# Fourier front of a two-layer encoder: where the even halves of the mixer's output are added, and when the third even weight is split

## The chip, the cores and the metric

The kernel runs on one core of a Trainium2 chip. The time is the device time of the whole program in microseconds (us), as a median of several runs. The profile is of one execution. Its engines are PE (TensorE matmuls), PEld (TensorE weight loads), DVE (VectorE), ACT (ScalarE), POOL (GpSimd) and SP (SyncE, which here only issues transfers). L12 is line 12 of the kernel that the profile shows.

## The reference

Two sequences of 512 tokens with 1024 features go through two layers. Layer 0 mixes tokens by a 2-D Fourier transform, layer 1 by grouped attention; each is followed by a squared-ReLU MLP. The change lies in layer 0's mixer.

```python
def fourier_mix(h, w_out):
    B, S, _ = h.shape
    hg = h.astype(jnp.float32).reshape(B, S, N_FGROUPS, F_GROUP)
    f = jnp.fft.fft2(hg, axes=(1, 3), norm="ortho").real
    f = f.reshape(B, S, D_MODEL).astype(h.dtype)
    return f @ w_out

def trunk(x, ...):
    for i in range(DEPTH):
        if i % N_MIXERS == 0:
            x = x + fourier_mix(rms_norm(x, fourier_norm[j]), fourier_w_out[j])
        else:
            x = x + gqa_attention(rms_norm(x, attn_norm[j]), ...)
        x = x + sq_relu_mlp(rms_norm(x, mlp_norm[i]), mlp_w_up[i], mlp_w_down[i])
    return rms_norm(x, final_norm)
```

All of it is float32. Most products split each operand into a rounded high part and the rest, the low part, and take three matmuls (high x high, high x low, low x high).

## The kernel before

The front (layer 0's mixer) is written out by hand: inside `tc.manual_schedule` each engine runs its instructions in the order of the code, and waits only for data, buffers and transfers. PE first transforms sequence 0, then takes its products with the output weight, transforms sequence 1 (`transform`) and takes its products, and then starts layer 0's MLP, whose first products are at L1039. After that nothing is part of the change.

The transform's result is symmetric in the tokens up to a sign, so the product with the weight falls into an even half (257 token columns, from the sums of weight rows, `we`) and an odd half (255 columns, from the differences, `wo`). Output column n gets even + odd, its mirror column, n + 256 in the kernel's token order, even - odd. A `Fold` j = 0 to 3 makes a quarter of these weights: `minus` forms the difference on DVE and adds the other rows into the raw weight by an accumulating transfer (POOL L694), `even_hi` casts the sum to its high part (ACT L711), and `even_lo` subtracts for the low part (DVE L714).

The residual `xs[q, i]` holds feature tiles 2i and 2i+1 of sequence q, one pair, [128, 2, 512]. For sequence 0 it is put together in steps:

- `odd_put` copies an odd product from PSUM into the pair, plain (ACT L777) and negated into the mirrored columns (L778).
- `add_input` adds the layer's input to the pair by an accumulating transfer on POOL's queue (L801), pairs in the order 2, 0, 3, 1.
- `even_put` copies the even product from PSUM to `even_part[i]` (ACT L786); for pairs 0 and 1 it copies a second time into the mirrored columns (L788).
- `add_even` adds `even_part[i]` to the pair: pairs 0 and 1 by an accumulating transfer from SBUF to SBUF (POOL L793), pairs 2 and 3 on DVE (L796, which reads the even half twice through a broadcast, and L798 for the two edge columns).

Accumulating transfers into one pair have to wait for each other. Between the folds and the input adds stand POOL's L440 transfers, which fold sequence 1's own input (after DVE's L431 and L444). When a pair is complete, `square` squares its tiles on ACT (L180) and POOL adds them up (L184). PE reduces the sum over the partitions (`root`, L193), DVE and ACT make the inverse root (L141 to L146), and PE spreads it over the partitions (`spread`, L201, copied by ACT L202) for the MLP's norm.

Sequence 1's transform calls `hook1` after each sequence part ("seq", 0 to 3) and feature stage ("feat", 0 to 3); its order is seq 0, 1, 2, feat 0, seq 3, feat 1, 2, 3. After each part its result is split by ACT and DVE at L86 and L87, the high part by ACT and the low part by DVE, which also sets PSUM banks free. The last split of the transform is `nyq_out` (ACT L596, DVE L597), which the last matmul (L754) of each even product reads. `hook1` places the squares, the later pair adds, sequence 1's loads (`load_xs`, SP L168, held until the square given as `made` is done) and the first put-aways (L214) and MLP weight loads (L101) among these steps. Sequence 1's even products then go to `xs[1, i]` by DVE (L765, L766), after which the odd ones follow (L770, L771).

Of the kernel before, what the change touches and what calls it, by code (L numbers as in the profile page):

```python
# [16 lines left out]
ALU = mybir.AluOpType  # L17
# [27 lines left out]
def trunk_kernel(ctx, tc, x_in, xt_in, y_out, tables, rope, gfour, gcol, grow, gfin,  # L45
                 w_four, w_nyq, w_qkv, w_o, w_a22, w_up, w_row2, w_row4, w_sum2, w_sum4, w_down):
    nc = tc.nc
# [17 lines left out]
    def slot(shape, dt):  # L65
        return act.tile(shape, dt, tag="u4", name=nm("u"))

    def tm(shape=(P, 512), dt=F32):
        return tmp.tile(list(shape), dt, tag="t2", name=nm("t"))
# [29 lines left out]
    def load_raw(src, shape=(P, 1024)):  # L99
        raw = rawp.tile(list(shape), F32, tag="raw", name=nm("raw"))  # L100
        nc.sync.dma_start(raw, src)  # L101
        return raw
# [62 lines left out]
    def load_xs(q, src, after=None):  # L165
        for i in range(4):
            xs[q, i] = slot([P, 2, 512], F32)
            made = nc.sync.dma_start(xs[q, i], src[i])  # L168
            if after is not None:
                behind(made, after, sync=True)  # L170

    def xt(q, fo):
        return xs[q, fo // 2][:, fo % 2]

    def square(q, fo, n=512, alone=False, first=0):

        if fo == first:
            acc[q] = tm()
        s = acc[q] if fo == first else tm()
        made = nc.scalar.activation(s[:, :n], xt(q, fo)[:, :n], AF.Square)  # L180
        if alone:
            apart[q] = s
        elif fo != first:
            nc.gpsimd.tensor_add(acc[q][:, :n], acc[q][:, :n], s[:, :n])  # L184
        return made
# [27 lines left out]
    def put_away(q, i):  # L213
        nc.sync.dma_start(park[q, i], xs[q, i])  # L214
# [542 lines left out]
    def even_outs(q, fos):  # L757
        return outs(q, fos, we, 0, 258, (wn.w, un[q]))

    def odd_outs(q, fos):  # L760
        return outs(q, fos, wo, 256, 256)
# [13 lines left out]
    def odd_put(q, fo, o):  # L775
        x = xt(q, fo)
        nc.scalar.copy(x[:, 1:256], o[:, 1:256])  # L777
        nc.scalar.activation(x[:, 257:], o[:, 1:256], AF.Copy, scale=-1.0)  # L778

    even_part = {}  # L780

    def even_put(q, fo, o):
        i, f = fo // 2, fo % 2
        if f == 0:
            even_part[i] = slot([P, 2, 512], F32)
        nc.scalar.copy(even_part[i][:, f, :257], o[:, :257])  # L786
        if i < 2:
            nc.scalar.copy(even_part[i][:, f, 257:], o[:, 1:256])  # L788

    def add_even(q, i):  # L790
        x, e = xs[q, i], even_part[i]
        if i < 2:
            nc.gpsimd.dma_start(x, e, accum_op=ALU.add)  # L793
            return
        both = x.rearrange("p f (h n) -> p f h n", h=2)[:, :, :, 1:]
        nc.vector.tensor_add(both, e[:, :, 1:256].unsqueeze(2).broadcast_to([P, 2, 2, 255]), both)  # L796
        edge = x[:, :, 0:257:256]
        nc.vector.tensor_add(edge, e[:, :, 0:257:256], edge)  # L798

    def add_input(q, i):  # L800
        nc.gpsimd.dma_start(xs[q, i], xt_in[q][i], accum_op=ALU.add)  # L801

    ET = mybir.EngineType
    with tc.manual_schedule(engines={ET.PE, ET.Activation, ET.DVE, ET.Pool, ET.SP}):
# [19 lines left out]
        fold = [Fold(0)]  # L824
# [63 lines left out]
        order = [4, 5, 6, 7, 0, 1, 2, 3]  # L888
        o = dict(zip(order, odd_outs(0, order)))
# [12 lines left out]
        fold[1].even_hi()  # L902
        fold[1].even_lo()
        g0.chain(5, 6)
        for fo in order[:2]:
            odd_put(0, fo, o[fo])
        for j in range(2, 4):
            fold[j].even_hi()
            fold[j].even_lo()
        g0.gain(1)  # L910
        g0.minus(1)
        g0.plus_there(1)
        for fo in order[2:]:
            odd_put(0, fo, o[fo])
        for i in range(2):
# [5 lines left out]
        g1.gain(1)  # L921
        g1.minus(1)
        g1.plus_there(1)
        for i in (2, 0, 3, 1):
            add_input(0, i)
        g1.squares(1)
        g1.chain(1, 2)
        e = even_outs(0, range(3))
        for fo in range(2):
            even_put(0, fo, e[fo])  # L930
        add_even(0, 0)

        def even(fo):
            even_put(0, fo, even_outs(0, [fo])[0])
# [6 lines left out]
        g0.split_odd()  # L941
        g1.chain(4, 6)
        even_put(0, 2, e[2])
        for i in range(2):
            g1.scale(slice(i, i + 1))
        even(3)
        add_even(0, 1)
        even(4)
        g1.combine()
        g1.split_hi()  # L950
        g1.split_lo()
        for fo in range(5, KC):
            even(fo)
        add_even(0, 2)

        raws = []
        blocks = Blocks(0)

        def hook1(at, j):
            if at == "seq":  # L960
                if j < 3:
                    made = square(0, order[j], first=4)
                if j == 0:
                    add_even(0, 3)
                elif j == 1:
                    load_xs(1, xt_in[1], made)
                    put_away(0, 2)
                    raws.extend(load_raw(w_up[0, 2 * p]) for p in range(4))
            else:
                square(0, order[3 + j], first=4)  # L970
                if j == 3:
                    square(0, order[7], first=4)

        transform(1, hook1)
        for fo in range(KC):
            e, = even_outs(1, [fo])
# [561 lines left out]
    def qkv(cg, q, t, ws, k0=0, k1=KC, o=None):  # L1538
        o = ps() if o is None else o
        cols = slice(t * P, (t + 1) * P)  # L1540
        for k in range(k0, k1):
            w = ws[k // 2]
            c = (k % 2) * 512
            mm3(o, hT[q][k][:, 0, cols], hT[q][k][:, 1, cols],
                w[0][:, c : c + 512], w[1][:, c : c + 512], k == 0, k == KC - 1)
        return o
# [62 lines left out]
    def transpose_q(q, h):  # L1609
        pt = ps()  # L1610
        c = (h % 2) * HD
        for t in range(NT):
            nc.tensor.transpose(pt[:, t * P : (t + 1) * P], qr[q, h // 2][:, t, c : c + HD], ident)  # L1613
        qT = slot([P, 2, 512], F32R)
        split(qT[:, 0], qT[:, 1], pt)
        return qT
# [150 lines left out]
    with tc.manual_schedule(engines={ET.Activation, ET.DVE}):  # L1767
        for cg in (2, 0, 1):
            later = next_ws({2: 0, 0: 1}[cg]) if cg != 1 else iter(())
            for q in range(NSEQ):  # L1770
# [6 lines left out]
                for t in range(NT if (cg, q) != (1, 1) else 2):  # L1777
                    if (cg, q, t) == (1, 1, 0):
                        first = transpose_q(0, 0)
# [19 lines left out]
    with tc.manual_schedule(engines={ET.Activation}):  # L1799
        o = qkv(1, 1, 2, ws[1])  # L1800
# [6 lines left out]
        o = qkv(1, 1, 3, ws[1])  # L1807
# [34 lines left out]
    todo, e, rows = heads_out.plain_sums(), [tm() for _ in range(4)], []  # L1842
# [13 lines left out]
    with tc.manual_schedule(engines={ET.PE}):  # L1856
        o = {}
# [12 lines left out]
        o = {}  # L1870
# [24 lines left out]
        o, lows = {}, []  # L1895
# [89 lines left out]
    with tc.manual_schedule(engines={ET.PE, ET.Activation, ET.DVE, ET.Pool, ET.SP}):  # L1985
# [17 lines left out]
        x, z = xtok  # L2003
# [3 lines left out]
        def tile(t, c0, c1, at=0, mid=lambda: None):  # L2007
            o = ps()[:, : c1 - c0]
            for k in range(len(ats)):
                ak, wk = ats[k][1], ws[k]  # L2010
                cols = slice(t * P, (t + 1) * P)
                mm3(o, ak[0][:, cols], ak[1][:, cols], wk[0][:, c0:c1], wk[1][:, c0:c1], k == 0, k == len(ats) - 1)
                if k == at:
                    mid()
            return o
# [11 lines left out]
        o = [tile(2, 0, 512, 2, ob.root)]  # L2027
# [8 lines left out]
        o = [tile(3, 0, 512)]  # L2036
# [183 lines left out]
```

## Time and profile before

| | |
|---|---|
| runs | 1683.16, 1678.90, 1682.27 us; median 1682.27 us |
| profiled execution | 1682.66 us, span 1680.9 us, mean granted clock 0.998 |
| busy, share of the span | PE 1662.8 us (99%), PEld 83%, DVE 75%, ACT 52%, POOL 23% |
| chain that ended last | PE 93%, DMA 2%, DVE 2%, ACT 1%, issue 1% |
| input adds L801 | 4 transfers of 512 KB, issued from 48.6 to 55.7 us |
| even transfers L793 | 2 of 512 KB, issued at 59.2 and 64.7 us, landing after 8.7 and 10.3 us |
| first MLP product (L1039) | starts at 100.86 us |

A timeline row has the start, the length, the engine, the line, the operation, out<-in, shapes and a count; in brackets stands how long the engine was idle before it and what is held to have ended that. A landing is the time from a transfer's issue to its end. The releaser of a wait is inferred: where the one named had long been done, it was another, often a transfer.

### The profile page before, as it was taken

The numbers are of one execution on the slowest core, as the hardware profiler recorded it, in microseconds if no ns is written. First come the engines' busy times: TensorE is split into PE (matmuls) and PEld (weight loads), VectorE is DVE, ScalarE is ACT, GpSimd is POOL, SyncE is SP. The second block draws the span as 40 slices with busy tenths as digits, with TensorE's granted clock in tenths as the row PEclk, the third lists the DMA queues.
The fourth block names the chain that finished last, engine by engine and source line by source line (L and its number), as shares of the span: only waits on it lengthen the run. The fifth ranks groups of instructions, "written<-read, shape, count | busy, mean of one in ns | idle before, by whom it ended". The sixth has DMA issues, their size and how long they took to land.

```text
span 1680.9 us, 22279 instructions
## 1 busy us (share of the span) xinstructions
PE 1662.8 (99%) x7827; PEld 1387.0 (83%) x7827; DVE 1265.0 (75%) x1855; ACT 873.2 (52%) x1546; POOL 394.5 (23%) x370
## 2 busy tenths in 40 slices
PE   9899999999999999999999999999999999999998
PEld 8788888888888888888888888888888888888887
DVE  8579787446877869868888977777855487878875
ACT  7665445446442435437688855554544552433334
POOL 3420543231000000424544312004422220000002
PEclk9999999999999999999999999999999999999999
DMA  9942555449865757525501146334544696756632
GB/s 311 268 146 85 201 188 184 167 168 336 298 224 162 232 171 236 187 72 173 188 14 39 64 163 225 123 116 160 210 155 156 221 375 198 234 159 217 192 105 101
DMA packets 122480, 303.53 MB, mean 181 GB/s; under 512 B 12376, under 2 KB 13528, under 8 KB 122368
## 3 DMA queue, kind: packets, MB, share of 16 engines
q1 hardware_dynamic: 98720, 253.53, 43.5%
q0 software_dynamic: 9248, 22.10, 6.3%
q10 hardware_dynamic: 14400, 26.48, 4.2%
q8 instruction: 61, 1.00, 0.2%
q14 instruction: 51, 0.42, 0.1%
HBM read 217.59 MB, written 82.38 MB: 178 GB/s over the span
## 4 chain that ended last, share of the span: by engine, by line
PE 93%; DMA 2%; DVE 2%; ACT 1%; issue 1%; POOL 0%; SPq 0%; DVEq 0%; POOLq 0%; ACTq 0%
PE ps L1039 73%; PE ps L81 6%; PE ps L83 6%; PE ps L82 6%; PE ps L1634 2%; DMA u<-u 1%; DMA u<-xt 1%; DMA u<-x 0%; PE ps L1613 0%; PE ps L193 0%; DMA raw<-w_sum 0%; DMA u<-spill_t 0%; DVE u L431 0%; DVE u L87 0%; ACT u L86 0%
## 5 line engine op out<-in xcount | busy, mean ns | idle before, releaser
L1039 PE MATMUL ps<-u,w 128*128 128x512 f32 x4944 | 1131.1, 389 | 0.0
L1039 PEld LDWEIGHTS ps<-u,w 128*128 128x128 f32 x4944 | 926.5, 188 | 195.1 <-ACT u L1072 1.7
L86 ACT CAST w<-raw 128x1024 fp32r<-128x1024 f32 (+1 forms) x216 | 213.6, 994 | 310.4 <-PE ps L1039 234.9
L87 DVE TENSOR_TENSOR w<-raw,w 128x1024 fp32r<-128x1024 f32 (+1 forms) x216 | 252.1, 1171 | 75.1 <-ACT w L86 74.8
L86 ACT CAST u<-u 128x1024 fp32r<-128x1024 f32 (+1 forms) x140 | 140.7, 1046 | 84.1 <-PE ps L1039 40.2
L87 DVE TENSOR_TENSOR u<-u,u 128x1024 fp32r<-128x1024 f32 (+1 forms) x140 | 169.0, 1237 | 18.8 <-ACT u L86 18.4
L1039 PE MATMUL ps<-u,u 128*128 128x512 f32 x600 | 143.4, 390 | 0.3 <-DVE t L1249 0.3
L1276 POOL DMA_DIRECT2D raw<-w_sum x32 | 27.7, 866 | 469.0 <-DVE w L87 143.1
L1249 DVE TENSOR_TENSOR u<-ps,u 128x512 f32<-128x512 f32 x160 | 109.8, 688 | 37.0 <-PE ps L1039 34.5
L1157 POOL TENSOR_TENSOR u<-u 128x512 f32<-128x512 f32 x28 | 37.1, 1326 | 424.7 <-ACT u L1054 424.7
L1039 PEld LDWEIGHTS ps<-u,u 128*128 128x128 f32 x600 | 112.5, 188 | 24.5 <-DVE t L1249 0.7
L81 PE MATMUL ps<-u,u 128*128 128x512 f32 (+2 forms) x340 | 128.8, 381 | 2.8 <-DVE u L87 2.2
L184 POOL TENSOR_TENSOR t<-t,t 128x512 f32<-128x512 f32 (+1 forms) x54 | 79.4, 1474 | 190.0 <-ACT t L180 189.0
L83 PE MATMUL ps<-u,u 128*128 128x512 f32 (+2 forms) x340 | 123.8, 365 | 0.0
L82 PE MATMUL ps<-u,u 128*128 128x512 f32 (+2 forms) x340 | 123.7, 365 | 0.0
L1053 ACT ACTIVATE t<-t 128x512 f32<-128x512 f32 x64 | 40.5, 632 | 110.9 <-DVE t L1126 100.8
L81 PEld LDWEIGHTS ps<-u,u 128*128 128x128 f32 x340 | 64.4, 189 | 11.2 <-DVE u L87 1.8
L87 DVE TENSOR_TENSOR u<-ps,u 128x512 fp32r<-128x512 f32 (+3 forms) x112 | 68.0, 635 | 6.6 <-ACT u L86 6.0
L83 PEld LDWEIGHTS ps<-u,u 128*128 128x128 f32 x340 | 64.2, 189 | 10.5 <-DVE u L87 0.2
L82 PEld LDWEIGHTS ps<-u,u 128*128 128x128 f32 x340 | 64.4, 189 | 8.5 <-DVE u L87 0.5
L1113 DVE TENSOR_TENSOR t<-ps,u 128x512 f32<-128x512 f32 x32 | 22.1, 689 | 59.9 <-PE ps L1039 52.4
L180 ACT ACTIVATE t<-u 128x512 f32<-128x512 f32 (+1 forms) x64 | 37.9, 602 | 54.2 <-DVE u L1846 21.0
(282 smaller groups left out, 2051.7 us busy)
## 6 DMA issues: line engine op xcount, KB each, us to landing
raw<-w_up SPq DMA_DIRECT2D x80, 512.0 KB, 4.6
u<-spill_t SPq DMA_DIRECT2D x60, 512.0 KB, 6.8
raw<-w_sum SPq DMA_DIRECT2D x56, 512.0 KB, 5.4
u<-spill_b SPq DMA_DIRECT2D x45, 512.0 KB, 6.6
spill_t<-u SPq DMA_DIRECT2D x84, 256.0 KB, 2.0
spill_b<-t ACTq DMA_DIRECT2D x60, 256.0 KB, 4.4
raw<-w_row SPq DMA_DIRECT2D x28, 512.0 KB, 5.0
park<-u SPq DMA_DIRECT2D x24, 512.0 KB, 4.7
```

Source lines behind the costliest of these rows:

```text
L81: nc.tensor.matmul(out, lh, rh, start=first, stop=False)
L82: nc.tensor.matmul(out, lh, rl, start=False, stop=False)
L83: nc.tensor.matmul(out, ll, rh, start=False, stop=last)
L86: hi = nc.scalar.copy(dst_hi, src)
L87: return hi, eng.tensor_sub(dst_lo, src, f32(dst_hi))
L180: made = nc.scalar.activation(s[:, :n], xt(q, fo)[:, :n], AF.Square)
L184: nc.gpsimd.tensor_add(acc[q][:, :n], acc[q][:, :n], s[:, :n])
L1039: nc.tensor.matmul(o, w[x][:, sl], h[k][y], start=first and k + i == 0, stop=k == n - 1 and i == 2, skip_group_check=not first)
L1053: nc.scalar.activation(t, src, AF.Relu)
L1157: eng.tensor_sub(t[:, 0], b12, b11)
L1249: return nc.vector.tensor_add(x, o, x)
L1634: nc.tensor.transpose(pt[:, t * P : (t + 1) * P], probs[t][:, sc * P : (sc + 1) * P], ident)
```

## The change

`even_put` makes one copy for all pairs, and `add_even` adds all pairs on DVE; the two L793 transfers and the four L788 copies are gone. Pairs 0 and 1 are added after feat 0 and seq 3 of sequence 1's transform, among the low parts. The input adds go in the order 2, 3, 0, 1. Sequence 1's loads and what follows them on SP move from after seq 1 to after feat 0. The third even weight is split ahead of the first odd copies, the fourth behind the next gain and fold of sequence 1's input.

```diff
     def even_put(q, fo, o):
...
         nc.scalar.copy(even_part[i][:, f, :257], o[:, :257])
-        if i < 2:
-            nc.scalar.copy(even_part[i][:, f, 257:], o[:, 1:256])

     def add_even(q, i):
         x, e = xs[q, i], even_part[i]
-        if i < 2:
-            nc.gpsimd.dma_start(x, e, accum_op=ALU.add)
-            return
         both = x.rearrange("p f (h n) -> p f h n", h=2)[:, :, :, 1:]
...
         g0.chain(5, 6)
+        fold[2].even_hi()
+        fold[2].even_lo()
         for fo in order[:2]:
             odd_put(0, fo, o[fo])
-        for j in range(2, 4):
-            fold[j].even_hi()
-            fold[j].even_lo()
         g0.gain(1)
         g0.minus(1)
         g0.plus_there(1)
+        fold[3].even_hi()
+        fold[3].even_lo()
         for fo in order[2:]:
             odd_put(0, fo, o[fo])
...
-        for i in (2, 0, 3, 1):
+        for i in (2, 3, 0, 1):
             add_input(0, i)
...
         for fo in range(2):
             even_put(0, fo, e[fo])
-        add_even(0, 0)
...
         even(3)
-        add_even(0, 1)
         even(4)
...
                 if j == 0:
                     add_even(0, 3)
-                elif j == 1:
+                elif j == 3:
+                    add_even(0, 1)
+            else:
+                made = square(0, order[3 + j], first=4)
+                if j == 0:
+                    add_even(0, 0)
                     load_xs(1, xt_in[1], made)
                     put_away(0, 2)
                     raws.extend(load_raw(w_up[0, 2 * p]) for p in range(4))
-            else:
-                square(0, order[3 + j], first=4)
                 if j == 3:
                     square(0, order[7], first=4)
```

ACT where sequence 0's odd products are copied: u_441 and u_443 are pairs 2 and 3, the w are the high parts of the even weights, the raw and u_236 their sums. Before:

```order
L711 CAST w_572<-raw_228 128x1024
L777 COPY u_441<-ps_445 128x255
L778 ACTIVATE u_441<-ps_445 128x255
L777 COPY u_441<-ps_446 128x255
L778 ACTIVATE u_441<-ps_446 128x255
L711 CAST w_582<-raw_232 128x1024
L711 CAST w_585<-u_236 128x1024
L777 COPY u_443<-ps_447 128x255
```

With the change:

```order
L711 CAST w_572<-raw_228 128x1024
L711 CAST w_578<-raw_232 128x1024
L777 COPY u_441<-ps_445 128x255
L778 ACTIVATE u_441<-ps_445 128x255
L777 COPY u_441<-ps_446 128x255
L778 ACTIVATE u_441<-ps_446 128x255
L711 CAST w_590<-u_236 128x1024
L777 COPY u_443<-ps_447 128x255
```

The third cast stands ahead of the first four copies, so that only one cast is left between them and the other twelve.

POOL's queue at the input adds: u_437, u_439, u_441 and u_443 are pairs 0 to 3, t the squares. Before:

```order
L801 DMA u_441<-xt 128x1024
L801 DMA u_437<-xt 128x1024
L801 DMA u_443<-xt 128x1024
L801 DMA u_439<-xt 128x1024
L793 DMA u_437<-u_668 128x1024
L793 DMA u_439<-u_693 128x1024
L184 TENSOR_TENSOR t_841<-t_841,t_859 128x512
```

With the change (L801 has become L796):

```order
L796 DMA u_441<-xt 128x1024
L796 DMA u_443<-xt 128x1024
L796 DMA u_437<-xt 128x1024
L796 DMA u_439<-xt 128x1024
L184 TENSOR_TENSOR t_835<-t_835,t_853 128x512
```

Pair 3 has the second place and pair 0 the third; the sums of squares follow the input adds directly.

DVE in sequence 1's transform, from the lows of the first feature stage to those of the second. Before:

```order
L87 TENSOR_TENSOR u_907<-ps_896,u_907 128x257
L87 TENSOR_TENSOR u_907<-ps_897,u_907 128x255
L87 TENSOR_TENSOR u_931<-ps_915,u_931 128x258
L87 TENSOR_TENSOR t_932<-ps_916,t_932 128x256
L87 TENSOR_TENSOR u_948<-ps_937,u_948 128x257
L87 TENSOR_TENSOR u_948<-ps_938,u_948 128x255
```

With the change (L796 and L798 have become L791 and L793):

```order
L87 TENSOR_TENSOR u_884<-ps_873,u_884 128x257
L87 TENSOR_TENSOR u_884<-ps_874,u_884 128x255
L791 TENSOR_TENSOR u_437<-u_668,u_437 128x4x255
L793 TENSOR_TENSOR u_437<-u_668,u_437 128x4
L87 TENSOR_TENSOR u_927<-ps_911,u_927 128x258
L87 TENSOR_TENSOR t_928<-ps_912,t_928 128x256
L791 TENSOR_TENSOR u_439<-u_690,u_439 128x4x255
L793 TENSOR_TENSOR u_439<-u_690,u_439 128x4
L87 TENSOR_TENSOR u_946<-ps_935,u_946 128x257
L87 TENSOR_TENSOR u_946<-ps_936,u_946 128x255
```

Pairs 0 and 1 stand behind the first feature stage's lows and behind the last sequence part's; the lows of the other three feature stages follow them.

## The prediction

> **What bounds the kernel now.** I read the page first, then TensorE's (PE's) waits, the chain of waits, and the engines' timelines from 32 to 101 us, where every edit lies.
>
> ```profile
> PE 1662.8 (99%) x7827; PEld 1387.0 (83%) x7827; DVE 1265.0 (75%) x1855; ACT 873.2 (52%) x1546; POOL 394.5 (23%) x370
> ```
>
> PE is busy over nearly the whole span, so time can only come out of stretches where it stands or runs slowly. PE's waits from 36 to 84 us (line, releaser: total, times, longest):
>
> ```profile
> PE ps L193 <- POOL t L184: 3.8, 1, 3.8
> PE ps L81 <- DVE u L87: 1.6, 1, 1.6
> PE ps L81 <- ACT u L786: 0.6, 1, 0.6
> PE ps L81 <- ACT u L778: 0.5, 1, 0.5
> ```
>
> The chain of waits (start, us, what) shows what stood behind the longest: the second even transfer, whose pair is then squared on ACT, summed (POOL L184) and reduced by PE (L193).
>
> ```profile
> 64.73 10.30 DMA u<-u
> ...
> 75.89 1.28 POOL t L184
> ...
> 78.55 1.05 PE ps L193 x8
> ```
>
> Two rows of the table by stretches (stretch, length, busy time and count of PE, PEld, DVE, ACT, POOL, then granted clock, DMA share, GB/s):
>
> ```profile
> 78.50:84.80 6.30, 6.25 (x40) 6.25 (x41) 1.43 (x6) 3.60 (x8) 0.00 (x0) 0.73 0.94 382
> 84.80:101.00 16.20, 16.20 (x137) 16.20 (x136) 15.82 (x25) 9.12 (x11) 2.62 (x2) 1.00 0.22 66
> ```
>
> And three rows of PE's timeline, the first two and the last matmul of sequence 1's first even output:
>
> ```profile
> 67.36 0.28 PE L81 MATMUL ps<-u,w 128*128 128x258 f32 x1
> 67.48 0.29 PE L82 MATMUL ps<-u,w 128*128 128x258 f32 x1
> ...
> 71.25 0.39 PE L754 MATMUL ps<-u,u 72*128 72x258 f32 x1
> ```
>
> Unhindered, matmuls start 0.12 us apart (67.36 to 67.48). The 12 steps to L754 should take 1.45 us and took 3.89, so this output loses 2.4. After the 3.8 us stop the clock was 0.73 for 6.3 us: 6.3 x 0.27 = 1.7 us. From 84.8 to 101 PE is full, and DVE nearly so. Lost before 84.8 us: 0.5 + 0.6 + 1.6 + 2.4 + 3.8 + 1.7 = 10.6 us. That is the ceiling of the gain.
>
> **Third even weight earlier.** ACT's rows, DVE's row, POOL's issue of the third fold (L694) and the landing of the four folds:
>
> ```profile
> 32.79 1.98 ACT L711 CAST w<-raw 128x1024 fp32r<-128x1024 f32 x2
> 37.11 0.37 ACT L777 COPY u<-ps 128x255 f32<-128x255 f32 x1 [2.33 <-PE ps L83]
> 39.28 1.23 DVE L714 TENSOR_TENSOR w<-raw,w 128x1024 fp32r<-128x1024 f32 x1 [1.53 <-ACT w L711]
> 24.15 0.88 POOL L694 DMA_DIRECT2D raw<-w_four  x1 [0.35 <-DVE u L693]
> DMA to landing us min/median/max: 7.4/8.5/10.0
> 39.30:47.20 7.90, 7.41 (x62) 7.21 (x61) 7.80 (x9) 7.87 (x21) 2.44 (x4) 1.00 0.81 221
> ```
>
> The cast (1.98 / 2 = 0.99 us) goes into ACT's 2.33 us gap from 34.8, DVE's subtraction into its 1.53 us gap. The raw weight lies there by 24.15 + 10.0 = 34.2 at the worst, so the move can't cost. The later odd copies come one cast earlier, which covers the 0.5 us bank wait on L778: bounds 0 and 0.5, I take 0.5. DVE is full from 39.3 to 47.2 (7.80 of 7.90), so its gain-and-fold products, the L440 transfers that wait for them and the input adds queued on POOL behind these come up to 1.5 us earlier: bounds 0 and 1.5, I take 1.5.
>
> **Single copies.** Four copies go from ACT:
>
> ```profile
> L788 ACT COPY u<-ps x4: 372/374/393, 47.3 to 53.0; 128x255 f32<-128x255 f32 x4
> ```
>
> 4 x 0.374 = 1.5 us of ACT work. PE's 0.6 us bank wait on L786 hangs on ACT reaching the last even copies, and ACT is now earlier by 1 to 1.5: bounds 0 and 0.6, I take 0.6. With both steps PE enters sequence 1's transform 1.1 us earlier.
>
> **Two transfers out, and the order 2, 3, 0, 1.** POOL's queue (start, length, line), DVE's stop for pair 3, ACT's stop for pair 0, and the landing of the four input adds (L801):
>
> ```profile
> 59.20 0.87 POOL L793 DMA_DIRECT2D u<-u  x1 [2.61 <-ACT u L86]
> 64.73 0.86 POOL L793 DMA_DIRECT2D u<-u  x1 [4.66 <-ACT u L86]
> 61.03 1.22 DVE L796 TENSOR_TENSOR u<-u,u 128x1020 f32<-128x1020 f32 x1 [2.39 <-DMA u<-xt]
> 68.00 0.63 ACT L180 ACTIVATE t<-u 128x512 f32<-128x512 f32 x1 [2.46 <-DMA u<-u]
> DMA to landing us min/median/max: 6.8/8.6/9.5
> ```
>
> Each L793 has to wait for the input add of its own pair, and the copies printed as its releaser are early ones; I read 59.2 and 64.7 as the landings of the second and the fourth add. The third landed at 61.0, where DVE stopped waiting. In the new order pair 3 has the second place, pair 0 the third, pair 1 the fourth as before. Less 1.5 us they are there at 57.7, 59.5 and 63.2. Beside the fourth there are two 512 KB transfers less; I count nothing for it. ACT's 2.46 us stop, which made the lows of the last feature stages late, goes with the transfer into pair 0. On POOL only the L184 sums stand behind L793; they come free earlier.
>
> **Two more pair adds on DVE.** What DVE has to run there in its written order, one row of each kind:
>
> ```profile
> 57.86 0.43 DVE L87 TENSOR_TENSOR u<-ps,u 128x258 fp32r<-128x258 f32 x1 [0.19 <-ACT u L86]
> 62.24 0.42 DVE L87 TENSOR_TENSOR u<-ps,u 128x258 fp32r<-128x258 f32 x1
> 62.58 0.42 DVE L87 TENSOR_TENSOR t<-ps,t 128x256 fp32r<-128x256 f32 x1
> 65.23 0.77 DVE L87 TENSOR_TENSOR u<-ps,u 128x257 fp32r<-128x257 f32 x2
> 70.78 0.42 DVE L597 TENSOR_TENSOR u<-ps,u 16x258 fp32r<-16x258 f32 x1
> 98.98 1.66 DVE L257 TENSOR_TENSOR u<-u,u 128x1024 fp32r<-128x1024 f32 x1
> 98.01 1.55 POOL L184 TENSOR_TENSOR t<-t,t 128x512 f32<-128x512 f32 x1 [19.52 <-ACT t L180]
> ```
>
> A pair add is 1.21 us (61.03 to 62.24), a low 0.34 (62.24 to 62.58), two feature lows 0.77, the Nyquist low 0.42. POOL's sums run beside the new adds. In the last two rows DVE worked from SBUF beside such a sum and took 1.66 instead of 1.22, so I put 0.44 on each of the two new pairs (bounds 0 and 0.9 together). With PE 1.1 us earlier: lows of the first part from 56.8 to 57.5; pair 3 from its landing at 57.7 to 58.9, the 2.39 us stop gone and with it PE's 1.6; four lows to 60.3; first feature lows to 61.0; pair 0 to 62.7; two lows to 63.4; pair 1 to 65.0; three feature pairs to 67.3; Nyquist to 67.7.
>
> PE could begin its even output at 67.36 - 2.7 = 64.7, but its L754 needs the Nyquist low: 67.7 instead of 71.25. That is 3.5 of the first 5.1 us; 1.6 us of new waiting stays, behind the two added pairs.
>
> The Trainium skill ("SBUF — State Buffer", Who interferes with whom) says that a DVE instruction with two SBUF inputs and a GpSimd instruction that reads SBUF exclude each other, the later one standing until the other is through. By that each new pair could stand for a whole sum of 1.28 us, 2.6 us in place of 0.9, and the gain would be 1.7 us smaller. The 1.66 us row agrees in kind: it began inside the POOL row and was held for no more than the rest of it.
>
> The squares of pair 1 follow its add at 65.0 and end near 67, the two POOL sums (1.28 each, 1.55 when shared) near 70. PE reaches L193 27 matmuls after L754, at 67.7 + 27 x 0.12 = 70.9. So the 3.8 us wait goes with nearly 1 us to spare, and the slow clock's 1.7 us with it.
>
> **Sequence 1's loads** stand behind square 7 instead of square 5. SP's issue, the landing of the four and of the first alone, and the first and last step of the root that PE's L201 waits for:
>
> ```profile
> 59.81 2.77 SPq L168 DMA_DIRECT2D u<-xt  x4
> u<-xt SPq DMA_DIRECT2D x4, 512.0 KB, 10.7
> u<-xt SPq DMA_DIRECT2D x1, 512.0 KB, 8.3
> 79.64 0.16 DVE L141 TENSOR_SCALAR s<-ps 128x4 f32<-128x4 f32 x1 [4.09 <-PE ps L193]
> 80.74 0.16 DVE L146 SCALAR_TENSOR_TENSOR s<-ps,s 128x4 f32<-128x4 f32 x1
> ```
>
> I estimate issues from 60.8 on, one later than now by 1 us, 0.7 apart. At 8.3 us, the first's time, two lie there at 69.1 and 69.8 and hold up only DVE. At the median of 10.7 it is 71.5 and 72.2: three additions of 0.77 end at 73.8, the root's 1.26 us at 75.1, and PE, at L201 from 70.9 + 1.05 + 13 x 0.12 = 73.5, waits 1.6. The crowd is 1 MB smaller, so I take 8.3, no cost. SP's put-aways no longer wait for the two transfers.
>
> **Sum.** 3.5 + 3.8 + 1.7 = 9.0 us. Behind 84.8 us the instructions keep their order and should move as a whole. The profiled execution took 1682.66 us, 0.39 above the median of the runs, 1682.27: 1682.66 - 9.0 = 1673.7.
>
> **Rivals.**
>
> *Data late.* The 1.5 us at the front don't come, and pair 1 and all behind it are 1.5 later; or the loads take 10.7 and cost 1.6; or both, with the loads later too, 4.6. Gain 4.4 to 7.5, time 1675.2 to 1678.3. For: the DMA share is still 0.94 in the row from 78.5. Against: less is moved.
>
> *POOL's sums hold DVE to their full length.* 1.7 us less: gain 7.3, 1675.4. For: the stretched row. Against: it lost a third of a sum, not one.
>
> *The gain is given back by 101 us.* DVE is busy 15.82 of 16.20 us there. If it enters 4 us or more later than PE, PE runs dry by as much: gain 0 to 5, 1677.7 to 1682.7. Against: nothing is added to that stretch.
>
> *Slower: DVE stands in its order on the fourth landing.* The lows of three feature stages now stand behind pair 1, where only a square did. If the fourth add lands at T, L754 comes at T + 1.2 + 0.4 + 2.7 = T + 4.3, and the point now at 84.8 follows 13.6 - 5.5 = 8.1 later. The kernels are even at T = 72.4; from 77.4 the new one loses over 5 us, and T = 80 gives 1690.3. For: a 10.30 us landing stands in the chain. Against: T was 64.7 with more traffic.
>
> That the change does none of what it says would need another cause of the L193 wait; the chain runs through the removed transfer without a break.
>
> **Numbers.** Chances: forecast (gain 7.5 to 10.6) 0.57, data late 0.15, POOL 0.08, given back 0.13, slower 0.07. A measurement of this kernel can tell about 0.3%, 5 us, from no change. Faster by more: 0.57 + 0.08 + 0.12 of the late data = 0.77. Within: 0.13 + 0.03 = 0.16. Slower: 0.07. Forecast, late data and POOL hold 0.80: from the ceiling, 1672.1, less 2.6 for the runs' own spread (1678.9 to 1683.16), up to 1678.3: 1669.5 to 1678.5.
>
> **What would show it.** Right: no L793, a wait at L193 under 1 us, a clock of 1.00 through sequence 1's even outputs, the first L754 near 67.7, L1039's first product near 92 instead of 101, and no gap ahead of DVE's third L714. Wrong: DVE standing ahead of a pair add or of the first L765 for a load; a root that is late at L201; or products that start early and a span that keeps its length.

## The result, and the profile after

The changed kernel takes 1675.0 us (median of six runs, 1673.8 to 1675.8), the kernel before 1682.1 in the same comparison: ratio 0.9959, 95% interval 0.9946 to 0.9972, 7 us faster. The profiled execution took 1675.20 us, span 1673.4. The page's first part and PE's waits from 36 to 84 us (line, releaser: total, times, longest):

```profile
PE 1660.7 (99%) x7827; PEld 1385.5 (83%) x7827; DVE 1267.7 (76%) x1859; ACT 872.2 (52%) x1542; POOL 392.4 (23%) x368
```

```profile
PE ps L82 <- DVE u L87: 2.1, 2, 1.6
PE ps L81 <- ACT u L786: 1.1, 1, 1.1
```

The 3.8 us at L193 is gone, and so are the waits at L778 and for pair 3. New are 2.1 us for lows of DVE, and the bank wait on L786 has grown. By stretches (columns as in the prediction's table; from L193 on, and up to the first MLP product):

```profile
72.60:77.30 4.70, 4.70 (x42) 4.70 (x42) 2.18 (x8) 2.24 (x5) 0.00 (x0) 1.00 1.03 415
77.30:93.30 16.00, 16.00 (x135) 16.00 (x135) 15.65 (x24) 9.12 (x11) 2.45 (x2) 1.00 0.36 132
```

The granted clock is 1.00 where it was 0.73. From PE's timeline:

```profile
67.54 0.39 PE L82 MATMUL ps<-u,w 128*128 128x258 f32 x1 [1.58 <-DVE u L87]
...
69.32 0.39 PE L754 MATMUL ps<-u,u 72*128 72x258 f32 x1
...
72.66 0.95 PE L193 MATMUL ps<-ones,t 128*128 128x2 f32 x8
...
93.34 0.86 PE L1036 MATMUL ps<-u,w 128*128 128x512 f32 x3
```

The first product (L1036 now, L1039 before) starts 7.52 us earlier, and the span is 7.5 shorter: nothing is given back behind it. Where the predicted 9.0 fell short shows in DVE's timeline (pairs 3, 0 and 1, wide addition and edge addition) and POOL's beside it:

```profile
57.65 1.21 DVE L791 TENSOR_TENSOR u<-u,u 128x1020 f32<-128x1020 f32 x1
58.78 0.16 DVE L793 TENSOR_TENSOR u<-u,u 128x4 f32<-128x4 f32 x1
...
60.91 1.80 DVE L791 TENSOR_TENSOR u<-u,u 128x1020 f32<-128x1020 f32 x1
62.63 1.25 DVE L793 TENSOR_TENSOR u<-u,u 128x4 f32<-128x4 f32 x1
...
64.47 1.20 DVE L791 TENSOR_TENSOR u<-u,u 128x1020 f32<-128x1020 f32 x1
65.59 1.23 DVE L793 TENSOR_TENSOR u<-u,u 128x4 f32<-128x4 f32 x1
```

```profile
58.96 4.89 POOL L184 TENSOR_TENSOR t<-t,t 128x512 f32<-128x512 f32 x3 [4.60 <-ACT t L180]
64.73 6.16 POOL L184 TENSOR_TENSOR t<-t,t 128x512 f32<-128x512 f32 x4 [0.88 <-ACT t L180]
```

Pair 3, with POOL idle, takes 57.65 to 58.85, 1.20 us. Pair 0 takes 60.91 to 63.80, 2.89; pair 1 takes 64.47 to 66.75, 2.28. The two pay 1.69 + 1.08 = 2.77 us for POOL's company, and the edge addition of 128 x 4 numbers takes 1.25 us instead of 0.16. The chain of waits shows the standing, as "issue":

```profile
60.99 0.65 DVE u L791
61.64 0.99 issue
62.63 0.20 DVE u L793
62.83 0.97 issue
63.80 0.41 DVE u L87
```

### The profile page after: what moved, and what is told of

It reads as the page before. It is cut to its first block, busy times and chain, and to the rows that moved or that the text cites. A ratio compares the mean times of both kernels' runs of the same rounds, so it can differ in the third digit from the quotient of the medians.

```text
span 1673.4 us, 22274 instructions
## 1 busy us (share of the span) xinstructions
PE 1660.7 (99%) x7827; PEld 1385.5 (83%) x7827; DVE 1267.7 (76%) x1859; ACT 872.2 (52%) x1542; POOL 392.4 (23%) x368
## 3 DMA queue, kind: packets, MB, share of 16 engines
q0 software_dynamic: 8960, 21.05, 6.0%
## 4 chain that ended last, share of the span: by engine, by line
PE 95%; DVE 2%; DMA 1%; ACT 1%; issue 1%; SPq 0%; POOL 0%; DVEq 0%; ACTq 0%; POOLq 0%
PE ps L1036 74%; PE ps L82 6%; PE ps L81 6%; PE ps L83 6%; PE ps L1631 2%; DVE u L87 0%; DMA u<-x 0%; PE ps L1610 0%; PE ps L193 0%; DMA raw<-w_sum 0%; DMA u<-u 0%; PE ps L534 0%; PE ps L537 0%; DVE u L703 0%; DVE w L714 0%
## 5 line engine op out<-in xcount | busy, mean ns | idle before, releaser
L1036 PE MATMUL ps<-u,w 128*128 128x512 f32 x4944 | 1130.8, 389 | 0.0
L1036 PEld LDWEIGHTS ps<-u,w 128*128 128x128 f32 x4944 | 926.6, 188 | 194.6 <-ACT u L1069 1.7
L86 ACT CAST w<-raw 128x1024 fp32r<-128x1024 f32 (+1 forms) x216 | 213.7, 995 | 310.3 <-PE ps L1036 233.3
L87 DVE TENSOR_TENSOR w<-raw,w 128x1024 fp32r<-128x1024 f32 (+1 forms) x216 | 251.3, 1167 | 75.2 <-ACT w L86 75.0
L86 ACT CAST u<-u 128x1024 fp32r<-128x1024 f32 (+1 forms) x140 | 140.7, 1047 | 84.6 <-PE ps L1036 34.9
L87 DVE TENSOR_TENSOR u<-u,u 128x1024 fp32r<-128x1024 f32 (+1 forms) x140 | 168.5, 1233 | 16.7 <-ACT u L86 16.2
L1036 PE MATMUL ps<-u,u 128*128 128x512 f32 x600 | 143.7, 390 | 0.4 <-DVE t L1246 0.4
L1036 PEld LDWEIGHTS ps<-u,u 128*128 128x128 f32 x600 | 112.4, 188 | 24.8 <-DVE t L1246 1.1
L87 DVE TENSOR_TENSOR u<-ps,u 128x512 fp32r<-128x512 f32 (+3 forms) x112 | 67.7, 633 | 3.2 <-ACT u L86 2.8
L86 ACT CAST u<-ps 128x512 fp32r<-128x512 f32 (+3 forms) x112 | 58.8, 556 | 7.5 <-PE ps L1631 6.1
```

Source lines behind the costliest of these rows:

```text
L86: hi = nc.scalar.copy(dst_hi, src)
L87: return hi, eng.tensor_sub(dst_lo, src, f32(dst_hi))
L1036: nc.tensor.matmul(o, w[x][:, sl], h[k][y], start=first and k + i == 0, stop=k == n - 1 and i == 2, skip_group_check=not first)
```

## The experiments

For all kernels I read four marks: the start of DVE's first L714, of its first 128x258 low (L87) of sequence 1, of PE's first L754 and of the first MLP product. *Front*, *middle* and *rest* are the times between them. DVE's two marks in the changed kernel, and the first in the kernel before (its next two stand in the prediction):

```profile
34.43 1.22 DVE L714 TENSOR_TENSOR w<-raw,w 128x1024 fp32r<-128x1024 f32 x1
...
56.95 0.43 DVE L87 TENSOR_TENSOR u<-ps,u 128x258 fp32r<-128x258 f32 x1 [0.18 <-ACT u L86]
```

```profile
35.06 1.22 DVE L714 TENSOR_TENSOR w<-raw,w 128x1024 fp32r<-128x1024 f32 x1
```

| kernel | median us | ratio to before, 95% | front | middle | rest |
|---|---|---|---|---|---|
| before | 1681.6 to 1682.1 | | 22.80 | 13.39 | 29.61 |
| changed | 1675.0 | 0.9959 (0.9946 to 0.9972) | 22.52 | 12.37 | 24.02 |
| changed, again | 1674.75 | 0.9959 (0.9947 to 0.9972) | 22.05 | 12.37 | 24.04 |
| e1 edges on POOL | 1674.95 | 0.9958 (0.9946 to 0.9971) | 22.31 | 11.34 | 24.05 |
| e2 no sums | 1671.54 | 0.9942 (0.9929 to 0.9954) | 21.57 | 9.61 | 24.06 |
| e3 third weight back | 1675.5 | 0.9966 (0.9952 to 0.9979) | 22.81 | 12.51 | 25.01 |
| e4 front back | 1676.29 | 0.9969 (0.9958 to 0.9981) | 22.81 | 12.52 | 25.10 |
| e5 order 2, 0, 3, 1 | 1676.39 | 0.9969 (0.9958 to 0.9979) | 21.16 | 14.30 | 25.54 |
| e6 pair 1 alone | 1675.6 | 0.9964 (0.9951 to 0.9977) | 22.83 | 12.63 | 24.14 |
| e7 pair 0 alone | 1682.37 | 1.0006 (0.9996 to 1.0015) | 22.83 | 17.71 | 26.43 |
| e8 late fourth | 1681.79 | 1.0000 (0.9990 to 1.0009) | 22.84 | 18.40 | 24.82 |
| e9 edges early | 1672.66 | 0.9949 (0.9936 to 0.9963) | 21.83 | 9.90 | 26.63 |
| e11 pair 0 back | 1674.49 | 0.9959 (0.9947 to 0.9972) | 21.74 | 12.72 | 24.06 |
| e12 edges, later root | 1674.41 | 0.9961 (0.9948 to 0.9975) | 22.06 | 9.90 | 24.05 |

The ratio is to the kernel before on the same chip. e1 to e4 ran on one chip, e5 to e8 on a second, e9 to e11 and the changed kernel's second measurement on a third, e12 on a fourth.

Theory A: the missing 1.6 us is DVE standing for POOL's sums. Theory B: late data or the front's order sets the end.

**Is it POOL? (e2)** In `square`, for sequence 0:

```diff
-        elif fo != first:
+        elif fo != first and q != 0:
             nc.gpsimd.tensor_add(acc[q][:, :n], acc[q][:, :n], s[:, :n])
```

> The changed kernel with POOL's additions of sequence 0's squares in this stage left out (later norms' sums of sequence 0 too), so that the root there reduces one tile alone: part of the computation is left out. Theory A: all wide pair additions take 1.21, all edge additions 0.16; pair 0 done at 62.1 instead of 63.8, pair 1 at 64.0 instead of 66.75; first L754 near 66.6 instead of 69.3; the second matmul of the even output waits under 0.3 for DVE instead of 1.58; the start of the feed-forward's first product 2.7 us earlier than 93.3. Its whole time can fall by more than that, since seven POOL additions of every later norm of sequence 0 go too, so that the stage's rows decide. Theory B: L754 within 0.5 of 69.3.

DVE's additions of pairs 0 and 1:

```profile
59.80 1.21 DVE L791 TENSOR_TENSOR u<-u,u 128x1020 f32<-128x1020 f32 x1
60.93 0.16 DVE L793 TENSOR_TENSOR u<-u,u 128x4 f32<-128x4 f32 x1
...
61.67 1.21 DVE L791 TENSOR_TENSOR u<-u,u 128x1020 f32<-128x1020 f32 x1
62.80 0.16 DVE L793 TENSOR_TENSOR u<-u,u 128x4 f32<-128x4 f32 x1
```

The middle falls by 2.76 us, as much as the two pairs had paid. Theory A is shown. L754, at 65.45, came earlier than expected because the front was 0.95 shorter too, which is another matter (below).

**The edge additions (e1, e9).** e1, in `add_even`:

```diff
-        nc.vector.tensor_add(edge, e[:, :, 0:257:256], edge)
+        (nc.gpsimd if i < 2 else nc.vector).tensor_add(edge, e[:, :, 0:257:256], edge)
```

> The changed kernel with the two 128x4 edge additions of pairs 0 and 1 on POOL instead of VectorE (DVE). Theory A (the missing 1.6 us of the first term is DVE standing for POOL's sums, most of it at the edge additions: 1.25 and 1.23 us where pair 3's took 0.16): pair 0 is done on DVE at 62.7 instead of 63.8 and pair 1 some 2.1 us earlier than 66.75, near 64.6; sequence 1's first L754 near 67.2 instead of 69.3; time 1.6 to 2.2 us under the changed kernel, about 1673. The wide addition of pair 0 still stretches (near 1.8 us). Theory B (data, or the order of the front, sets the end): L754 stays within 0.5 of 69.3, time as the changed kernel, 1675.

Half of it came: L754 at 68.19. POOL's timeline and ACT's square of pair 0 show why:

```profile
63.72 1.34 POOL L793 TENSOR_TENSOR u<-u,u 128x4 f32<-128x4 f32 x2
```

```profile
64.94 0.63 ACT L180 ACTIVATE t<-u 128x512 f32<-128x512 f32 x1 [2.28 <-POOL u L793]
```

POOL's edge additions, begun at 63.72, now stood for DVE's wide addition of pair 1 (63.19, 1.64 long), ACT's square for the edge, and DVE's lows for ACT. The exclusion works both ways. Of the 1.10 us by which the first product was earlier, 0.1 was left at 1644 us. A drift of nearly that size needs no cause in the edit: the changed kernel run again moves against its first profile by 0.8 us between 721 and 1644 us. e9 therefore puts the edges ahead of the sums that hold them; `add_edge` is the edge addition alone, taken out of `add_even` for pairs 0 and 1:

```diff
                 if j == 0:
+                    add_edge(nc.gpsimd, 0, 0)
                     add_even(0, 3)
...
             else:
+                if j == 0:
+                    add_edge(nc.gpsimd, 0, 1)
                 made = square(0, order[3 + j], first=4)
```

> The changed kernel with the edge additions of pairs 0 and 1 on POOL and ahead of the sums that would hold them: pair 0's before POOL's first sum, pair 1's after the second. In the run with the edges on POOL behind the third sum, POOL's edge of pair 0 stood for VectorE's wide addition of pair 1 and ACT's square for the edge (2.28 us), so that the lows came late from ACT. Theory A with that mended: wide additions of pairs 0 and 1 of 1.6 to 1.8 each, ACT's stop under 1.2, VectorE's lows without a wait for ACT, first L754 near 67.3 (68.2 there, 69.3 in the changed kernel), the first product near 91.4; time 1673 to 1674 if later stages keep it. If ACT or PE set the end instead: L754 at 68.2 or later, time as the changed kernel.

The middle is 9.90, 2.47 under the changed kernel's, and L754 comes at 65.98. In the profiled execution PE then runs into POOL (the row of L754 is that of the third even output), and the clock falls behind that:

```profile
69.21 0.28 PE L754 MATMUL ps<-u,u 72*128 72x258 f32 x1
70.30 1.05 PE L193 MATMUL ps<-ones,t 128*128 128x2 f32 x8 [0.81 <-POOL t L184]
```

```profile
72.00:76.00 4.00, 4.00 (x23) 4.00 (x22) 1.13 (x5) 2.02 (x4) 0.00 (x0) 0.58 1.02 415
```

Still this has the lowest median of the kernels that do all the work, 1672.66, 2.1 under the changed kernel on the same chip; the intervals overlap, so that it is better is likely and not settled.

**A later root on top (e12).**

```diff
-            if fo == 2:
+            if fo == 3:
                 blocks.root(0)
-            if fo == 3:
+            if fo == 4:
                 blocks.spread(0)
```

> The kernel with the early edges on POOL, and in it sequence 0's root (L193) and its spreading (L201) one even output later. The profiled execution there still stood 0.81 at L193 for POOL's last sum, and the granted clock was 0.58 from 72 to 76, 1.7 us. With the root 13 matmuls (1.56 us) later: no wait at L193, clock 1.00, the first product 2.5 us earlier than 92.6, near 90.1, if that stop is what the clock fell for. VectorE, full from 77 to 96 in all of these kernels, gets its first normalising products 1 us earlier than there at most; where it is the next to set the end, the gain stays under 1 and the time at 1672 to 1672.7, otherwise 1671 to 1671.5.

In the profiled execution the clock stayed at 1.00 and the first product came at 90.39, as expected. Then PE stood at an MLP product (L1043) for ACT's copy of an earlier one out of PSUM (L1076), and ACT had stood ahead of it for an MLP weight:

```profile
109.50 0.95 PE L193 MATMUL ps<-ones,t 128*128 128x2 f32 x8
112.10 3.06 PE L1043 MATMUL ps<-u,w 128*128 128x512 f32 x12 [1.65 <-ACT u L1076]
```

```profile
110.00 1.04 ACT L86 CAST w<-raw 128x1024 fp32r<-128x1024 f32 x1 [1.06 <-DMA raw<-w_up]
...
111.48 0.57 ACT L1076 COPY u<-ps 128x512 f32<-128x512 f32 x1
```

1.7 of 2.95 us were given back there. The next thing to be late is the MLP's weight stream, not DVE as I had written; 1674.41 is no better than the changed kernel.

**One part at a time (e6, e7, e11).** e6 is the kernel before with pair 1 alone added by DVE, after seq 3; e7 with pair 0 alone, after feat 0. For e6 (e7 has `i == 1`, and `add_even(0, 0)` moves):

```diff
-        if i < 2:
+        if i == 0:
             nc.gpsimd.dma_start(x, e, accum_op=ALU.add)
...
-        add_even(0, 1)
...
+                elif j == 3:
+                    add_even(0, 1)
```

> The kernel before with one part of the change alone: pair 1 is added by VectorE in the lows of sequence 1, pair 0 still by transfer. The 3.8 us wait at L193 goes and with it the 1.7 us of slow clock; the first even output is later by the pair addition. With the addition sized as predicted (1.21 + 0.44): L754 at 72.9 instead of 71.25, gain 5.5 - 1.65 = 3.9, time 1678.2. Theory A (its edge addition stands for a whole sum, 2.3 to 2.9 us together): L754 73.5 to 74.2, gain 2.6 to 3.2, time 1679 to 1679.5.

> The kernel before with the other part alone: pair 0 is added by VectorE, pair 1 still by transfer. ACT's 2.46 us stop goes; the transfer into pair 1 is issued near 64.7 as before, with 0.5 MB less under way beside it. If its length is set by the crowd: 6 to 8 us instead of 10.3, L193 from 74.5 to 76.5 instead of 78.55, gain 2 to 4. If not: L193 stays at 78 to 79, and the gain is 0 to 1. Either way a wait of over 1 us stays at L193, and the clock falls behind it: this part alone does not bring the 3.8 + 1.7.

Pair 1 alone brings 6.1 us (0.9964 of 1682). Both sizes of the expectation were wrong: L754 came at 70.06, not later than 71.25. The addition cost nothing, since the lows behind it had to wait for ACT all the same, which had stood for pair 0's transfer, here until 66.81 (68.00 in the kernel before). The edge addition did not stand either: POOL had no sum to run between 65.5 and 67.9. ACT's and DVE's timelines of e6:

```profile
66.81 0.63 ACT L180 ACTIVATE t<-u 128x512 f32<-128x512 f32 x1 [1.66 <-DMA u<-u]
```

```profile
64.75 1.81 DVE L796 TENSOR_TENSOR u<-u,u 128x1020 f32<-128x1020 f32 x1
66.49 0.15 DVE L798 TENSOR_TENSOR u<-u,u 128x4 f32<-128x4 f32 x1
...
67.74 0.76 DVE L87 TENSOR_TENSOR u<-ps,u 128x257 fp32r<-128x257 f32 x2 [0.43 <-ACT u L86]
```

Pair 0 alone brings nothing. The transfer into pair 1 took as long as before with less beside it (queue issue, KB, landing), and the wait for it showed up at another place: as the profile names it, ACT stood for it at the Nyquist split, and PE's L754 with ACT and DVE.

```profile
u<-u POOLq DMA_DIRECT2D x1, 512.0 KB, 10.4
```

```profile
73.92 0.37 ACT L596 CAST u<-ps 72x258 fp32r<-72x258 f32 x1 [5.94 <-DMA u<-u]
```

```profile
74.80 0.58 PE L754 MATMUL ps<-u,u 72*128 72x258 f32 x1 [5.74 <-DVE u L597]
```

The Nyquist split does not read pair 1; that it needs a buffer which the transfer still held is likely and was not tested, so e7 has a wait that no other kernel has. Without it there was still little to win: POOL's last two sums, which need pair 1, ended at 77.6 instead of 78.5.

e11 takes pair 0's half out of the changed kernel (pair 0's doubled copies come back too):

```diff
...
+        if i == 0:
+            nc.gpsimd.dma_start(x, e, accum_op=ALU.add)
+            return
...
-        for i in (2, 3, 0, 1):
+        for i in (2, 0, 3, 1):
             add_input(0, i)
...
+        add_even(0, 0)
...
                 if j == 0:
-                    add_even(0, 0)
```

> The changed kernel with pair 0 added by transfer again, in its old place and with the input order 2, 0, 3, 1 and its doubled copies: third weight, single copies of pair 1 and pair 1's addition stay. If nearly the whole gain is pair 1's (the kernel before with that alone took 1675.6): time 1674.8 to 1676, VectorE standing about 2.2 for the third landing, no L193 wait, edge addition of pair 1 0.16. By the prediction's terms (1.6 of the wait at the first lows and ACT's 2.46 stop come back, less 1.65 of a pair addition): 0 to 1.5 slower than the changed kernel.

1674.49 against 1674.75: moving pair 0 is worth nothing. e11's DVE at pair 3:

```profile
58.37 2.14 DVE L796 TENSOR_TENSOR u<-u,u 128x1020 f32<-128x1020 f32 x1 [1.45 <-DMA u<-xt]
```

There DVE stood 1.45 for the third landing, and 0.93 more inside this row, beside a sum of POOL's. With pair 0 moved and the order 2, 3, 0, 1 both go, and pair 0 pays 1.69 under POOL's sums instead.

**The order of the input adds (e5).**

```diff
-        for i in (2, 3, 0, 1):
+        for i in (2, 0, 3, 1):
             add_input(0, i)
```

> The changed kernel with the input adds issued in the order 2, 0, 3, 1 again, so that pair 3 has the third place. By the prediction's landings (59.5 for the third place): VectorE stands ahead of pair 3 from 57.65 to 59.5, all behind it is 1.9 later, less what the stretch under POOL's sums gives back; L754 70.5 to 71.2, time 1 to 2 us over the changed kernel. By the issues in the trace of after (third at 49.5, slowest landing 9.3): a stop of 1.2 at most, L754 70 to 70.5, time 0.5 to 1.2 over it. If landings were no limit: no stop, no change.

```profile
58.61 1.40 DVE L791 TENSOR_TENSOR u<-u,u 128x1020 f32<-128x1020 f32 x1 [2.19 <-DMA u<-xt]
```

The stop is back, the middle 1.9 longer, the time 1.4. The 1.4 is not the price of the order alone: in this profile the front was 1.36 shorter, and the rest 1.5 longer by a slow clock (last section). The third landing is at 58.6; the prediction had 59.5.

**The front (e3, e4, e10).** e3 puts the third and fourth weight back where they were; e4 also has the doubled copies again; e10 is the changed kernel itself.

```diff
-        fold[2].even_hi()
-        fold[2].even_lo()
         for fo in order[:2]:
             odd_put(0, fo, o[fo])
+        fold[2].even_hi()
+        fold[2].even_lo()
+        fold[3].even_hi()
+        fold[3].even_lo()
...
-        fold[3].even_hi()
-        fold[3].even_lo()
```

```diff
+        if i < 2:
+            nc.scalar.copy(even_part[i][:, f, 257:], o[:, 1:256])
```

> The changed kernel with the third even weight back behind the first odd outputs. By the prediction's steps (0.5 at the bank wait on L778, and the input adds 1.0 to 1.5 later): L778's wait of 0.5 returns, PE enters sequence 1 0.5 later, time about 0.5 above the changed kernel. Theory A as I read the trace of after: L778's wait returns (0.5) but the bank wait on L786 falls from 1.08 to about 0.6, since both end at the same copies; the input adds go out 1 us later and still land ahead of DVE; time within 0.3 of the changed kernel. Rival (data late): DVE stands ahead of pair 3, and the time grows by 1 or more.

> The changed kernel with both steps of the front undone: third even weight behind the first odd outputs, and the four doubled copies of pairs 0 and 1 back on ACT. By the prediction's steps 1.1 us (0.5 + 0.6) later into sequence 1 and 1.1 us slower. As I read the trace of after: 0.3 us at PE, time 0 to 0.5 above the changed kernel.

> The changed kernel again, beside the others on the same chip: 1674 to 1676; L754 near 69.3 (or up to 1.1 earlier if the second L440 transfer lands in time, as in two of the profiles of experiments); granted clock 1.00 in the stretch behind L754, if that belongs to this kernel and not to one execution.

L754 is 0.1 to 0.4 later in e3 and e4 than in the changed kernel's two profiles. Their first product is 1.4 later than in its first profile, 1.0 of it in the rest, where the clock was slow (last section); so their 0.5 and 1.3 us of time can't be put down to the front. Where the third weight stands as before, the front is 22.80 to 22.83 in five kernels, with single copies (e3) no shorter than with doubled ones (e4): the copies bring nothing. With the weight moved it is anything from 21.16 to 22.84. DVE's L490 decides, a step in folding sequence 1's input, which waits for an L440 transfer. In the changed kernel and in e9:

```profile
46.72 0.75 DVE L490 SCALAR_TENSOR_TENSOR u<-u,s,u 128x512 f32<-128x512 f32 x1 [1.46 <-DMA u<-u]
```

```profile
45.85 0.75 DVE L490 SCALAR_TENSOR_TENSOR u<-u,s,u 128x512 f32<-128x512 f32 x1 [0.77 <-DMA u<-u]
```

Front less this idle time is 21.06 in both, and 21.05 to 21.16 in all nine profiles with the weight moved (in three of them the profile names ACT, not the transfer, as what ended it). The move frees 1.75 us, and what L490 waits for, another length in each execution, takes 0 to 1.8 of it back.

**The slower rival (e8).** The input add of pair 1 goes out behind POOL's second sum:

```diff
-        for i in (2, 3, 0, 1):
+        for i in (2, 3, 0):
             add_input(0, i)
...
+                if j == 2:
+                    behind(add_input(0, 1), made, sync=True)
```

> The changed kernel with the input add of pair 1 issued behind the third square of pair 2 and 3's tiles, some 8 us later than now, to test the slower rival of the prediction: VectorE stands in its order on the fourth landing T, and L754 comes at T + 4.3. Issue near 61.6, landing 7 to 9 later: T = 68.6 to 70.6. By the rival L754 at 72.9 to 74.9; with the edge addition standing for a POOL sum up to 1.1 later. The first product then 24.0 behind L754, 96.9 to 100, or up to 1.7 later with a slow clock; time 1678.6 to 1683. If the fourth landing does not hold VectorE, nothing moves.

```profile
71.80 1.22 DVE L791 TENSOR_TENSOR u<-u,u 128x1020 f32<-128x1020 f32 x1 [6.88 <-DMA u<-xt]
```

DVE does stand in its order: the fourth landing T is at 71.8, L754 at 75.73 = T + 3.9 (T + 4.3 predicted), and the time is 1681.79 us, even with the kernel before. The prediction had put the point where the kernels are even at T = 72.4.

## Why the prediction was right, and where it was off

The sign, the mechanism of the larger part (the L193 wait and the clock behind it) and the range held; 1675.0 is 1.3 over the point. The gain of 7.1 us falls short of the 7.5 to 10.6 of the branch that had the chance of 0.57. What the runs bear out for the rest is the POOL rival (1675.4), which had 0.08.

- *3.8 + 1.7 at L193*: predicted 5.5, the rest shrank by 29.61 - 24.02 = 5.59. Right, and e6 shows that pair 1's transfer alone was its cause. (PE's waits in the prediction leave out one row of that view, 1.0 us for ACT's L86; it lies in the 2.4 of the first even output, so the sum stands.)
- *3.5 for the first even output*: L754 moved 71.25 - 69.32 = 1.93, of it 0.63 before any edit (the first L714), 0.28 in the front and 1.02 in the middle. The 0.63 is luck: that L714 starts anywhere from 34.25 to 35.14 in the other profiles, at 35.14 in the changed kernel's second. So 1.3 of the 3.5 came from the change. This is the term that failed, at two steps.
- Step one, *0.44 us for each pair added beside POOL's sums*, 0.9 together: they paid 2.77. I took 0.44 from one row that began inside a POOL sum, and counted one standing for each pair. A pair is two instructions, and each can be held again by whatever sum is running: the wide ones paid 0.59 and nothing, the edges 1.09 and 1.07. The Trainium skill's rule ("SBUF — State Buffer", Who interferes with whom), an exclusive lock on the shared read port, gave 2.6, and I gave it 0.08 although a row agreed in kind. The runs agree with it in both directions (e2, e1).
- Step two, *1.1 us at the front*: 0.28 in this profile, 0.75 in the second. The gap ahead of DVE's third L714 is gone and 1.75 us are freed, but the single copies brought nothing, and I did not ask what else L490 needs: the L440 transfer became the last to come.
- *Landings, loads*: the input adds went out 1.7 to 2.2 earlier (1.5 predicted), DVE stood for none of the three pairs, L765 waited only for PE, and L201 was not late. "Data late" did not happen.
- *Given back by 101 us*: not for this gain. For a larger one it did happen in the profile of e12, at 112 us.

## What to carry to other kernels

A VectorE addition with both inputs in SBUF, beside GpSimd sums, is priced per instruction and not by its size: here each stood for 0 to 1.1 us of a sum of 1.28. So count instructions, and put a short one where GpSimd is idle, or ahead of the sum. When a chain of waits ends in one transfer, take that transfer out first: here it was nearly the whole gain (6.1 of 7 us), and the second transfer, which the same idea removed, was worth nothing. An addition placed where its engine would have waited can cost nothing (e6), so look at what the engine was doing there before costing it.

## What the runs showed of the hardware that I had not expected

A slow clock does not need a long stop. After the same two waits (0.48 and 1.58 us, 1.57 in e3) the clock stayed at 1.00 in the changed kernel and fell to 0.50 in e3; rows of the two by stretches, the changed kernel first:

```profile
70.00:71.00 1.00, 1.00 (x11) 1.00 (x10) 0.50 (x2) 1.00 (x2) 0.89 (x1) 1.00 1.03 418
```

```profile
70.00:71.00 1.00, 1.00 (x6) 1.00 (x6) 0.75 (x2) 1.00 (x3) 1.00 (x1) 0.50 1.02 410
```

By half-microsecond stretches it is at half for 3.4 us each time in e3, e4, e5 and e9, from 68.8, 68.9, 70.6 and 72.7; the kernel before lost half of 3.4 too (1.7). With the two longest stops it is at half for twice as long: 6.8 us from 73.4 in e7 (a stop of 5.7, to 74.8) and 6.8 us from 70.9 in e8 (a stop of 7.5, to 73.8). The Trainium skill ("TensorE: Matmul & The Clock Gate", Part 1) has the gate judge activity in windows of about 3.4 us that run freely, not from the program's start. The length of the dips agrees, once or twice the 3.4. That a dip depends on where the windows fall would explain one clock for e3 and another for the changed kernel, but no run here moved the windows, so this stays argued. In a single execution the 1.7 us won back from the clock is then partly chance: a stop of 0.8 us at L193 was followed by a dip once (e9), waits of 1.6 were not in four profiles (the changed kernel twice, e6, e11). Over many runs the kernel before does lose more: the mean granted clock of a whole run is 0.996 to 0.998 in all 52 runs of the kernel before that were made beside the experiments, and 0.999 in nine of the changed kernel's eleven, 0.998 in the other two.
